# A tail of sixteen chunks: steps of three neighbouring chunks woven between the matmuls of one output tile, and the in-chunk weights by a predicated copy

## The chip, the cores and the metric

The kernel runs on one core of a Trainium2 chip. The metric is the device time of one execution in microseconds (us). TensorE (PE in the profile, PEld its weight loads), VectorE (DVE), ScalarE (ACT), GpSimd (POOL) and the DMA queues issued by SyncE (SP) work in parallel and wait for each other through semaphores.

## The reference, cut to what matters

Two layers of an encoder trunk over 2048 positions of width 1024. Each layer modulates its input, projects it, mixes it in two branches, and ends in `x <- LN(alpha * x + gate * W_out [branch 1 | branch 2])`. The change touches the end of the second layer: its second branch (a bidirectional state-space scan, SSD), its output projection and its last layer norm. What the second branch computes, with the backward direction as the same function on reversed time:

```python
seg = jnp.exp(jnp.where(mask, a_cum[..., :, None] - a_cum[..., None, :], -jnp.inf))
cb = jnp.einsum('bnigs,bnjgs->bgnij', cm, bm)
y = jnp.einsum('bgnij,bgrnij,bnjgrp->bnigrp', cb, seg, x)      # within a chunk
...
y = y + jnp.einsum('bnigs,bgrni,bngrps->bnigrp', cm, jnp.exp(a_cum), s_prev)   # from the carried state
...
x_fw, a_fw = dir_inputs(dt_f, 0)      # xs * dt, dt * -exp(a_log)
x_bw, a_bw = dir_inputs(dt_b, 1)
y = (ssd_chunked(x_fw, a_fw, bm, cm)
     + rev(ssd_chunked(rev(x_bw), rev(a_bw), rev(bm), rev(cm)))
     + d_skip.astype(jnp.float32)[:, None] * xs)
y = rms_norm(y.reshape(bsz, seq, WIDTH_D) * jax.nn.silu(dz.astype(jnp.float32)), ssm_norm_g)
```

Within a chunk of 128 positions both directions are one weight matrix of 128 by 128 for each of 8 heads: `w = E * cb * dt`, with the forward `dt` on one triangle, the backward `dt` on the other, and the sum of both on the diagonal, where `E` is 1.

## The kernel before, in words

The sequence is cut into 16 chunks (`NC`) of 128 positions. When the last input projection is done, these pieces are left, and they are the tail:

- `pass_b` (called through `other`) for two heads of the first branch, segments 1, 2 and 3 of 512 positions each. It ends in a store of the branch's rows of `y`, which the output tiles read back.
- `Ssd.local(c)`, for a chunk: four loads (`tk`, `bc`, `dzl`, `sbl`, lines 1228 to 1235), the product `pcb` (L1238), then for each of two groups of four heads the decay `E = exp(pd)` (POOL and ACT write `rr`, L1246 and L1249; four matmuls `pd`, L1250 and L1251; the exponential, L1253), the `dt` part of the weights (a scaled copy on ACT, L1256, and a `scalar_tensor_tensor` on DVE, L1257, for every head), and two products on DVE (L1259, L1260) that make `w`.
- `Ssd.forward(c)`: the matmuls `py` with `w` (L1273), the skip term (POOL, L1276), two state products `pin` (L1281) each with a DVE product (L1285) and a POOL sum (L1286), the state's update `pu` (L1211, from `xw`, L1203) into `sf` (L1220), the gate (L1292), the norm (L1294 to L1297), four transposes `pt` (L1300) and the result `syo` (L1302).
- `OutProj.steps(c)`, an output tile: 48 matmuls `oo` of 512 columns (L1032), half of them with the first branch's rows (`yr`, read back from memory), half with `syo`; each operand is split in a high part `yH` (L1003) and a low part `yL` (L1004). Then residual, statistics and layer norm (L1039 to L1050) and the store.

The order on each engine is not the written order: the framework plans it when the kernel is built, and of the instructions that are ready it takes the one written earliest. So what is written later fills gaps as far as its inputs and its buffers allow. Many buffers of the tail are single: the two halves of `rr` (tags T0, T1), `E` (cvt), `xw` (v), `syo` (kd), `yL`, and one PSUM bank for `pcb` and `pt` together. The written order before is, in the last loop (L1675 to L1680): `local(c + 1)` whole, at chunks 1, 5 and 9 a `pass_b` whole, `forward(c)` whole, tile c whole.

Of the kernel before, what the change touches and what calls it, by code (L numbers as in the profile page):

```python
# [10 lines left out]
F32 = mybir.dt.float32  # L11
F32R = mybir.dt.float32r
I32 = mybir.dt.int32
AF = mybir.ActivationFunctionType
ALU = mybir.AluOpType
AX = mybir.AxisListType
# [3 lines left out]
P = 128  # L20
# [261 lines left out]
def run(g):  # L282
    for _ in g:
        pass
# [32 lines left out]
def chained(*gs):  # L317
    for g in gs:
        yield from g
# [111 lines left out]
class Rec:  # L431
# [14 lines left out]
    def bank(self, name):  # L446
        return self.ps.tile([P, 512], F32, name=name, tag="rg", bufs=self.e.rg_bufs)
# [613 lines left out]
NC = S // P  # L1061


class Ssd:
# [157 lines left out]
    def local(self, c, pool, bank):  # L1222

        e, nc = self.e, self.e.nc
        cs = slice(c * P, (c + 1) * P)
        k = self.cur[c] = Env()
        kp = self.kp
        k.tk = kp.tile([P, 768], F32, name="tk", tag="tk", bufs=2)
        nc.sync.dma_start(k.tk, self.tok[cs, :])
        k.bc = kp.tile([P, 4, P], F32, name="bc", tag="cvx", bufs=2)  # L1230
        nc.sync.dma_start(k.bc, self.xc[:, :, cs])
        k.dz = kp.tile([P, 512], F32, name="dzl", tag="sb", bufs=2)
        nc.sync.dma_start(k.dz, self.dz[cs, :])
        k.sb = kp.tile([P, 512], F32, name="sbl", tag="cva", bufs=2)
        nc.sync.dma_start(k.sb, self.sbd[c])
        pcb = bank("pcb")
        for g in range(2):
            nc.tensor.matmul(pcb[:, g * P:(g + 1) * P], k.bc[:, g], k.bc[:, 2 + g], start=True, stop=True)  # L1238
        k.w = pool.tile([P, 2, 4, P], F32, name="w", tag="Q", bufs=2)
        for g in range(2):  # L1240
            pd = bank("pd")
            w = k.w[:, g]
            for d, (m1, m2) in enumerate((("gt", "le"), ("lt", "ge"))):
                r = pool.tile([P, 2, 4, P], F32R, name="rr", tag=f"T{d}", bufs=1)
                h0 = d * 8 + g * 4
                nc.gpsimd.tensor_tensor(r[:, 0], e.tri[m2].unsqueeze(1).broadcast_to([P, 4, P]),  # L1246
                                        self.aH[:, c, h0:h0 + 4].unsqueeze(2).broadcast_to([P, 4, P]), ALU.mult)
                for h in range(4):
                    nc.scalar.activation(r[:, 1, h], e.tri[m2], AF.Copy, scale=self.aL[:, c, h0 + h:h0 + h + 1])  # L1249
                nc.tensor.matmul(pd, e.trir[m1], r[:, 0], start=d == 0, stop=False)  # L1250
                nc.tensor.matmul(pd, e.trir[m1], r[:, 1], start=False, stop=d == 1)  # L1251
            E = kp.tile([P, 4, P], F32, name="E", tag="cvt", bufs=1)
            nc.scalar.activation(E, pd.rearrange("p (h i) -> p h i", h=4), AF.Exp)  # L1253
            for h in range(4):
                hh = g * 4 + h
                nc.scalar.activation(w[:, h], e.tri["le"], AF.Copy, scale=self.dt[:, c, hh:hh + 1])  # L1256
                nc.vector.scalar_tensor_tensor(w[:, h], e.tri["ge"], self.dt[:, c, 8 + hh:9 + hh], w[:, h],  # L1257
                                               ALU.mult, ALU.add)
            nc.vector.tensor_tensor(E, E, pcb[:, g * P:(g + 1) * P].unsqueeze(1).broadcast_to([P, 4, P]), ALU.mult)  # L1259
            nc.vector.tensor_tensor(w, w, E, ALU.mult)  # L1260

    def forward(self, c, pool, bank):
        e, nc = self.e, self.e.nc
        cs = slice(c * P, (c + 1) * P)
        h8 = lambda t: t.rearrange("p (h q) -> p h q", h=8)
        k = self.cur.pop(c)
        tk, bc, dz, sb = k.tk, k.bc, k.dz, k.sb
        if c == 0:
            self.sf = pool.tile([P, 512], F32, name="sf", tag="qm0", bufs=1)
            nc.gpsimd.memset(self.sf, 0.0)  # L1270
        py = bank("py")
        for hh in range(8):
            nc.tensor.matmul(py[:, hh * 64:(hh + 1) * 64], k.w[:, hh // 4, hh % 4], tk[:, hh * 64:(hh + 1) * 64],  # L1273
                             start=True, stop=True)
        acc = pool.tile([P, 512], F32, name="yacc", tag=f"{'kq'[c % 2]}m1", bufs=1)
        nc.gpsimd.tensor_tensor(h8(acc), h8(tk[:, :512]), self.dskip.unsqueeze(2).broadcast_to([P, 8, 64]), ALU.mult)  # L1276
        nc.vector.tensor_tensor(acc, py, acc, ALU.add)
        for d, st in ((0, self.sf), (1, sb)):
            po = bank("pin")
            for g in range(2):  # L1280
                nc.tensor.matmul(po[:, g * 256:(g + 1) * 256], bc[:, 2 + g], st[:, g * 256:(g + 1) * 256],  # L1281
                                 start=True, stop=True)
            t = pool.tile([P, 512], F32, name="ti", tag=f"Sf{d}", bufs=1)
            eq = self.ed["qf" if d == 0 else "qb"][:, c, :].unsqueeze(2).broadcast_to([P, 8, 64])
            nc.vector.tensor_tensor(h8(t), h8(po), eq, ALU.mult)  # L1285
            nc.gpsimd.tensor_tensor(acc, acc, t, ALU.add)  # L1286
        if c < NC - 1:
            pu = self.update(self.weighted(c, 0, tk, pool), tk[:, 512:], bank)
            new = pool.tile([P, 512], F32, name="sf", tag=f"{'kq'[c % 2]}m0", bufs=1)
            self.step(new, self.sf, c, 0, pu)  # L1290
            self.sf = new
        nc.vector.tensor_tensor(acc, acc, dz, ALU.mult)  # L1292
        ss = pool.tile([P, 1], F32, name="sss", tag="ss", bufs=4)
        nc.scalar.activation(t, acc, AF.Square, accum_out=ss)  # L1294
        nc.gpsimd.tensor_scalar(ss, ss, 1.0 / 512, 1e-6, ALU.mult, ALU.add)
        nc.gpsimd.tensor_tensor(ss, ss, e.mhalf[:, 0:1], ALU.pow)
        nc.scalar.activation(acc, acc, AF.Copy, scale=ss)  # L1297
        pt = bank("pt")
        for i in range(4):
            nc.tensor.transpose(pt[:, i * P:(i + 1) * P], acc[:, i * P:(i + 1) * P], e.ident)  # L1300
        yo = pool.tile([P, 4, P], F32, name="syo", tag="kd", bufs=1)
        nc.vector.tensor_tensor(yo, pt.rearrange("p (a b) -> p a b", a=4),  # L1302
                                self.gcol.unsqueeze(2).broadcast_to([P, 4, P]), ALU.mult)
        return yo

# [47 lines left out]
def trunk(ctx, tc, i, out):  # L1355
    nc = tc.nc
    e = Env()
# [5 lines left out]
    def const(name, shape, dt=F32):  # L1363
        t = cp.tile(list(shape), dt, name=f"c_{name}")
        nc.sync.dma_start(t, i[name])
        return t
# [63 lines left out]
    mp = opened("gla", "right")  # L1430
# [62 lines left out]
    def others():  # L1493
        for sg in (3, 2, 1, 0):
# [13 lines left out]
    mp = opened("na", "right")  # L1508
# [13 lines left out]
    op = OutProj(e, wp, lambda x, h: wwp.tile([P, ND // 2, D], F32R, name=f"wo{x}{h}"),  # L1522
                 lambda n: wp.tile([P, D], F32, name=n), obank, gated(e, wp, "yr", i["e_w_out"], gate), i["ln_g"][0], i["ln_b"][0], y, i["x"], x1)
# [13 lines left out]
    bank = banks(opened("pt1", "right", space=PSUM), "pt", 4)  # L1537
# [11 lines left out]
    hg = const("hgrn_g", [P, 1])  # L1549
    sg_ = const("ssm_g", [P, 4])  # L1550
    e.tri = {m: const(f"t_{m}", [P, P]) for m in TRI}
    e.trir = {}
    for m in ("gt", "lt"):
        e.trir[m] = cp.tile([P, P], F32R, name=f"r_{m}")
# [24 lines left out]
    kp = opened("conv", "left")  # L1579
    mp = opened("hgrn", "left")  # L1580
# [28 lines left out]
    sd = Ssd(e, sg_, dz, y[512:1024])  # L1609
# [19 lines left out]
    def other(h, sg, tags=None):  # L1629
        return pass_b(e, recs[h:h + 2], sg, mp, bbank, tags or [btags(t, sg % 2) for t in range(2)])  # L1630
# [33 lines left out]
    def sbank(name):  # L1664
# [2 lines left out]

    ftags = [{"qul": ("F", 2), "stwb": ("stw", 1), "sq": ("S320", 1), "og": ("KT", 1)},
             {"qul": ("F", 2), "stwb": ("stwb", 1, wp), "sq": ("S321", 1), "opl": ("uo", 1), "gt": ("q", 1)}]
    sd.local(0, mp, sbank)  # L1670
    sd.local(1, mp, sbank)
    op = OutProj(e, wp, lambda x, h: ip.hp.tile([P, ND // 2, D], F32R, name=f"wo{x}{h}", tag=f"h{'HL'[x]}{h}"),
                 lambda n: mp.tile([P, D], F32, name=n, tag="Kp", bufs=2), obank,
                 wout1, i["ln_g"][1], i["ln_b"][1], y, x1, out)
    for c in range(NC):  # L1675
        if 0 < c < NC - 1:
            sd.local(c + 1, mp, sbank)
        if c % 4 == 1 and c < 12:
            run(other(2, c // 4 + 1, ftags))
        op.tile(c, (4, 8), c == NC - 1, sd.forward(c, mp, sbank))  # L1680
    closed("po1", "pops1", "hp1", "hgrn", "hgrnps", "conv", "wb1", "hgrnc", "ssdc")


def layout(inp):

    f = lambda n: np.ascontiguousarray(inp[n])
    r = {}
# [28 lines left out]
    t, j = a[:, None], a[None, :]  # L1716
    for nm, m in (("gt", t > j), ("lt", t < j), ("le", t <= j), ("ge", t >= j)):
        r["t_" + nm] = m.astype(np.float32)
    lm = np.zeros((P, 5, 32), np.int32)
    i32 = np.arange(32)  # L1720
    for l in range(5):
# [21 lines left out]
```

## Time and profile before

| | us |
|---|---|
| median of 3 runs | 2748.59 (2747.47 to 2750.7) |
| the profiled execution, its own time | 2755.94 |
| its span in the trace | 2754.1 |
| PE busy | 2526.8 (92%) |
| DVE busy | 1493.4 (54%) |
| POOL busy | 1326.1 (48%) |
| ACT busy | 1122.9 (41%) |

Shares are of the whole span. The last matmul of the input projection starts at 2333.37, so the tail is the last 420 us or so. Times in the rows below are us from the span's start unless marked ns; PEclk is the granted TensorE clock as a share of full speed.

### The profile page before, as it was taken

Reading aid. Unit: us, or ns where it says so; the run is one execution under the profiler, and the core shown is the slowest. Engines: PE = TensorE matmul, PEld = TensorE weight load, DVE = VectorE, ACT = ScalarE, POOL = GpSimd, SP = SyncE. Lnnn points to the kernel's source line nnn. Section 1 sums busy time; section 2 is a strip of 40 time slices with the busy share of each in tenths; the row PEclk is TensorE's granted clock in tenths of the full one; section 3 lists DMA queues with packets and bytes.
Section 4 is the critical chain, followed back from the end, with each engine's and each line's share of the span. In section 5 each row is a group of like instructions: output and inputs, shape, how many; then the busy total and the mean of one; then the engine's idle time right before and its main releaser. Section 6 shows DMA issues by size and latency. Waiting matters only on the chain. (4 is left out here: it accounts for less than half of the span.)

```text
span 2754.1 us, 53110 instructions
## 1 busy us (share of the span) xinstructions
PE 2526.8 (92%) x20888; PEld 2125.2 (77%) x20888; DVE 1493.4 (54%) x2493; ACT 1122.9 (41%) x2355; POOL 1326.1 (48%) x1305
## 2 busy tenths in 40 slices
PE   7999999999999799998999999999999888788987
PEld 5877778887778677877788777888877677566776
DVE  6223335124433676765626356432625788687895
ACT  3152323244343644543323444232424453554652
POOL 4252325244442544434535556335534677575874
PEclk9999999999999899999999999999999999798998
DMA  8525434323365878775553335434436567543331
GB/s 275 159 99 169 145 115 132 115 95 106 109 221 181 253 210 234 202 205 167 173 201 126 106 124 177 136 127 131 134 105 207 169 200 235 182 148 112 117 115 62
DMA packets 269800, 432.46 MB, mean 157 GB/s; under 512 B 25936, under 2 KB 143600, under 8 KB 269552
## 3 DMA queue, kind: packets, MB, share of 16 engines
q1 hardware_dynamic: 267248, 420.69, 48.7%
q0 software_dynamic: 2304, 8.39, 0.8%
q8 instruction: 165, 2.70, 0.4%
q14 instruction: 83, 0.68, 0.1%
HBM read 296.60 MB, written 132.38 MB: 156 GB/s over the span
## 5 line engine op out<-in xcount | busy, mean ns | idle before, releaser
L186 POOL TENSOR_TENSOR wl<-wraw,wh 128x1024 fp32r<-128x1024 f32 (+2 forms) x116 | 290.5, 2524 | 293.9 <-ACT wh L185 293.0
L1032 PE MATMUL oo<-wo,yH 128*128 128x512 f32 x1024 | 309.9, 418 | 21.8 <-ACT yH L1003 20.2
L536 POOL TENSOR_TENSOR Kp<-Kp,T 128x256 f32<-128x256 f32 x144 | 125.7, 873 | 275.1 <-ACT F L492 111.7
L1032 PEld LDWEIGHTS oo<-wo,yH 128*128 128x128 f32 x1024 | 199.8, 201 | 65.3 <-ACT yH L1003 23.5
L860 POOL TENSOR_TENSOR nap<-nap,nasm 128x384 f32<-128x384 f32 (+2 forms) x128 | 115.7, 914 | 209.5 <-DVE nasm L859 192.2
L534 DVE TENSOR_TENSOR Kp<-Kp,T 128x256 f32<-128x256 f32 x144 | 103.7, 720 | 146.6 <-PE fine L459 60.2
L185 ACT CAST wh<-wraw 128x1024 fp32r<-128x1024 f32 (+2 forms) x116 | 116.8, 1052 | 154.5 <-PE obqk L205 27.4
L1032 PE MATMUL oo<-wo,yL 128*128 128x512 f32 x512 | 172.4, 405 | 3.0 <-DVE yL L1004 3.0
L532 DVE TENSOR_TENSOR Q<-Q,T 128x512 f32<-128x512 f32 x144 | 146.9, 1020 | 0.0
L885 PE MATMUL nay<-napts,nav 128*128 128x128 f32 (+1 forms) x832 | 121.5, 289 | 20.2 <-ACT napts L872 13.7
L885 PEld LDWEIGHTS nay<-napts,nav 128*128 128x128 f32 (+1 forms) x832 | 114.5, 202 | 31.3 <-ACT napts L872 16.1
L1154 DVE SCALAR_TENSOR_TENSOR cva<-cvx,cw,cva 128x512 f32<-128x512 f32 x96 | 104.2, 1098 | 30.5 <-ACT cva L1152 29.4
L1032 PEld LDWEIGHTS oo<-wo,yL 128*128 128x128 f32 x512 | 97.5, 193 | 23.5 <-DVE yL L1004 4.2
L205 PE MATMUL oqf<-hH,wh 128*128 128x512 f32 x256 | 104.8, 409 | 4.5 <-ACT wh L185 4.5
L205 PE MATMUL ox<-hH,wh 128*128 128x512 f32 x256 | 106.2, 415 | 0.0
L497 DVE COPY_PREDICATED S<-lmask,fine 128x128 f32<-128x128 int32 x160 | 43.7, 297 | 111.3 <-PE fine L459 111.2
L205 PE MATMUL ox<-hH,wl 128*128 128x512 f32 x256 | 102.7, 401 | 0.0
L205 PE MATMUL ox<-hL,wh 128*128 128x512 f32 x256 | 102.5, 400 | 0.0
L205 PE MATMUL oqf<-hL,wh 128*128 128x512 f32 x256 | 102.4, 400 | 0.0
L205 PE MATMUL oqf<-hH,wl 128*128 128x512 f32 x256 | 101.9, 399 | 0.5 <-POOL wl L186 0.5
L858 ACT ACTIVATE nap<-nap,namx 128x384 f32<-128x384 f32 (+2 forms) x128 | 79.2, 619 | 50.6 <-DVE namx L857 50.3
L156 POOL TENSOR_TENSOR hL<-hf,hH 128x512 fp32r<-128x512 f32 x36 | 50.2, 1403 | 96.9 <-ACT hH L155 96.9
(375 smaller groups left out, 7723.8 us busy)
## 6 DMA issues: line engine op xcount, KB each, us to landing
wraw<-in_o_w_dram SPq DMA_DIRECT2D x56, 512.0 KB
wraw<-in_e_w_dram SPq DMA_DIRECT2D x44, 512.0 KB
adw<-in_ada_w_dram SPq DMA_DIRECT2D x32, 512.0 KB
tk<-xtok SPq DMA_DIRECT2D x31, 384.0 KB
nat<-in_na_tab_dram SPq DMA_DIRECT2D x16, 640.0 KB
xt<-in_x_dram SPq DMA_DIRECT2D x16, 512.0 KB
adw<-in_ada_p_dram SPq DMA_DIRECT2D x16, 512.0 KB
naq<-aq SPq DMA_DIRECT2D x64, 128.0 KB
```

The lines of the kernel that those rows point to most:

```text
L156: (nc.vector if d % 2 and not act else nc.gpsimd).tensor_sub(hL[:, d, :], hf, hH[:, d, :].bitcast(F32))
L185: nc.scalar.copy(h[:, sl], raw)
L186: (nc.vector if e.wl_dve else nc.gpsimd).tensor_sub(l[:, sl], raw, h[:, sl].bitcast(F32))
L205: nc.tensor.matmul(oo, a, b, start=d == 0 and m == 0, stop=d == ND - 1 and m == 2)
L532: nc.vector.tensor_tensor(qv, qv, view(tcur, toff + 1, [[nb - 1, 2], [2, n2], [0, s]]), ALU.mult)
L534: nc.vector.tensor_tensor(kv, kv, view(tcur, toff + nb + 1, [[2, n2], [0, s]]), ALU.mult)
L536: nc.gpsimd.tensor_tensor(kv, kv, view(tcur, toff, [[2, n2], [0, s]]), ALU.mult)
L858: nc.scalar.activation(p[:, :nk], p[:, :nk], AF.Exp, bias=mx, scale=-1.0, accum_out=sm)
L860: nc.gpsimd.tensor_tensor(p[:, :nk], p[:, :nk], sm.broadcast_to([P, nk]), ALU.mult)
L885: nc.tensor.matmul(s.yp[:, n, :], b.vs[:kb, n, j, :], s.pts[n][:kb, j, :], start=j == 0, stop=j == nj - 1)
L1032: nc.tensor.matmul(os[n], ops[m][0][:, c, :], ops[m][1][c][:, ns], start=x == 0, stop=x == 23)
L1154: nc.vector.scalar_tensor_tensor(acc, xr[:, k:k + SW], cw[:, i, k:k + 1], acc, ALU.mult, ALU.add)
```

## The change

Four edits, all in the tail:

1. The weights within a chunk. Eight scaled copies (128x128) on ACT and eight `scalar_tensor_tensor` on DVE for a chunk become two copies (128x512) of the backward `dt` on ACT and two `copy_predicated` (128x512) on DVE, which put the forward `dt` where an integer mask `t_lei` is set. The diagonal then has the forward `dt` alone, so the backward `dt` times the diagonal of `pcb` is added to the skip factor: a product with the identity (`own`, DVE, 128x256 out of PSUM), a sum over it (`cd`), and two small products (`k.skip`, 128x8).
2. `local` and `forward` become generators of three steps each; `xw` is made at the end of `local` and not in `forward`.
3. `pass_b` for segments 1 to 3 becomes one generator of 12 steps.
4. The last loop has 17 turns. A turn c writes tile c-1 in its 24 steps of two matmuls, and between them: step 1 of `forward(c)` ahead of the first, step 2 ahead of the third, the three steps of `local(c + 1)` ahead of the 7th, 11th and 15th, one step of `pass_b` ahead of the 13th (turns 1 to 12), and step 3 of `forward(c)` (the transposes) ahead of the 21st.

```diff
@@ -1236,34 +1236,50 @@
         pcb = bank("pcb")
         for g in range(2):
             nc.tensor.matmul(pcb[:, g * P:(g + 1) * P], k.bc[:, g], k.bc[:, 2 + g], start=True, stop=True)
+
+        own = kp.tile([P, 2, P], F32, name="own", tag="cvt", bufs=1)
+        nc.vector.tensor_tensor(own, pcb[:, :2 * P].rearrange("p (g i) -> p g i", g=2),
+                                e.ident.unsqueeze(1).broadcast_to([P, 2, P]), ALU.mult)
+        cd = pool.tile([P, 2], F32, name="cd", tag="cd", bufs=2)
+        nc.vector.tensor_reduce(cd, own, AX.X, ALU.add)
+        k.skip = pool.tile([P, 2, 4], F32, name="skip", tag="skip", bufs=2)
+        nc.vector.tensor_tensor(k.skip, self.dt[:, c, 8:].rearrange("p (g h) -> p g h", g=2),
+                                cd.unsqueeze(2).broadcast_to([P, 2, 4]), ALU.mult)
+        nc.vector.tensor_tensor(k.skip, k.skip, self.dskip.rearrange("p (g h) -> p g h", g=2), ALU.add)
         k.w = pool.tile([P, 2, 4, P], F32, name="w", tag="Q", bufs=2)
         for g in range(2):
-            pd = bank("pd")
             w = k.w[:, g]
-            for d, (m1, m2) in enumerate((("gt", "le"), ("lt", "ge"))):
+            rs = []
+            for d, m2 in enumerate(("le", "ge")):
                 r = pool.tile([P, 2, 4, P], F32R, name="rr", tag=f"T{d}", bufs=1)
                 h0 = d * 8 + g * 4
                 nc.gpsimd.tensor_tensor(r[:, 0], e.tri[m2].unsqueeze(1).broadcast_to([P, 4, P]),
                                         self.aH[:, c, h0:h0 + 4].unsqueeze(2).broadcast_to([P, 4, P]), ALU.mult)
                 for h in range(4):
                     nc.scalar.activation(r[:, 1, h], e.tri[m2], AF.Copy, scale=self.aL[:, c, h0 + h:h0 + h + 1])
-                nc.tensor.matmul(pd, e.trir[m1], r[:, 0], start=d == 0, stop=False)
-                nc.tensor.matmul(pd, e.trir[m1], r[:, 1], start=False, stop=d == 1)
+                rs.append(r)
+            yield
+            pd = bank("pd")
+            for d, m1 in enumerate(("gt", "lt")):
+                nc.tensor.matmul(pd, e.trir[m1], rs[d][:, 0], start=d == 0, stop=False)
+                nc.tensor.matmul(pd, e.trir[m1], rs[d][:, 1], start=False, stop=d == 1)
             E = kp.tile([P, 4, P], F32, name="E", tag="cvt", bufs=1)
             nc.scalar.activation(E, pd.rearrange("p (h i) -> p h i", h=4), AF.Exp)
-            for h in range(4):
-                hh = g * 4 + h
-                nc.scalar.activation(w[:, h], e.tri["le"], AF.Copy, scale=self.dt[:, c, hh:hh + 1])
-                nc.vector.scalar_tensor_tensor(w[:, h], e.tri["ge"], self.dt[:, c, 8 + hh:9 + hh], w[:, h],
-                                               ALU.mult, ALU.add)
+            dts = [self.dt[:, c, d * 8 + g * 4:d * 8 + g * 4 + 4].unsqueeze(2).broadcast_to([P, 4, P]) for d in range(2)]
+            nc.scalar.copy(w, dts[1])
+            nc.vector.copy_predicated(w, e.lei.unsqueeze(1).broadcast_to([P, 4, P]), dts[0])
             nc.vector.tensor_tensor(E, E, pcb[:, g * P:(g + 1) * P].unsqueeze(1).broadcast_to([P, 4, P]), ALU.mult)
             nc.vector.tensor_tensor(w, w, E, ALU.mult)
+        if c < NC - 1:
+            k.xw = self.weighted(c, 0, k.tk, pool)
+        yield
 
     def forward(self, c, pool, bank):
+
         e, nc = self.e, self.e.nc
         cs = slice(c * P, (c + 1) * P)
         h8 = lambda t: t.rearrange("p (h q) -> p h q", h=8)
-        k = self.cur.pop(c)
+        k = self.cur[c]
         tk, bc, dz, sb = k.tk, k.bc, k.dz, k.sb
         if c == 0:
             self.sf = pool.tile([P, 512], F32, name="sf", tag="qm0", bufs=1)
@@ -1273,8 +1289,9 @@
             nc.tensor.matmul(py[:, hh * 64:(hh + 1) * 64], k.w[:, hh // 4, hh % 4], tk[:, hh * 64:(hh + 1) * 64],
                              start=True, stop=True)
         acc = pool.tile([P, 512], F32, name="yacc", tag=f"{'kq'[c % 2]}m1", bufs=1)
-        nc.gpsimd.tensor_tensor(h8(acc), h8(tk[:, :512]), self.dskip.unsqueeze(2).broadcast_to([P, 8, 64]), ALU.mult)
+        nc.gpsimd.tensor_tensor(h8(acc), h8(tk[:, :512]), k.skip.rearrange("p g h -> p (g h)").unsqueeze(2).broadcast_to([P, 8, 64]), ALU.mult)
         nc.vector.tensor_tensor(acc, py, acc, ALU.add)
+        yield
         for d, st in ((0, self.sf), (1, sb)):
             po = bank("pin")
             for g in range(2):
@@ -1285,7 +1302,7 @@
             nc.vector.tensor_tensor(h8(t), h8(po), eq, ALU.mult)
             nc.gpsimd.tensor_tensor(acc, acc, t, ALU.add)
         if c < NC - 1:
-            pu = self.update(self.weighted(c, 0, tk, pool), tk[:, 512:], bank)
+            pu = self.update(k.xw, tk[:, 512:], bank)
             new = pool.tile([P, 512], F32, name="sf", tag=f"{'kq'[c % 2]}m0", bufs=1)
             self.step(new, self.sf, c, 0, pu)
             self.sf = new
@@ -1295,13 +1312,15 @@
         nc.gpsimd.tensor_scalar(ss, ss, 1.0 / 512, 1e-6, ALU.mult, ALU.add)
         nc.gpsimd.tensor_tensor(ss, ss, e.mhalf[:, 0:1], ALU.pow)
         nc.scalar.activation(acc, acc, AF.Copy, scale=ss)
+        yield
         pt = bank("pt")
         for i in range(4):
             nc.tensor.transpose(pt[:, i * P:(i + 1) * P], acc[:, i * P:(i + 1) * P], e.ident)
         yo = pool.tile([P, 4, P], F32, name="syo", tag="kd", bufs=1)
         nc.vector.tensor_tensor(yo, pt.rearrange("p (a b) -> p a b", a=4),
                                 self.gcol.unsqueeze(2).broadcast_to([P, 4, P]), ALU.mult)
-        return yo
+        k.yo = yo
+        yield
 
 
 
@@ -1549,6 +1568,7 @@
     hg = const("hgrn_g", [P, 1])
     sg_ = const("ssm_g", [P, 4])
     e.tri = {m: const(f"t_{m}", [P, P]) for m in TRI}
+    e.lei = const("t_lei", [P, P], I32)
     e.trir = {}
     for m in ("gt", "lt"):
         e.trir[m] = cp.tile([P, P], F32R, name=f"r_{m}")
@@ -1667,17 +1687,23 @@
 
     ftags = [{"qul": ("F", 2), "stwb": ("stw", 1), "sq": ("S320", 1), "og": ("KT", 1)},
              {"qul": ("F", 2), "stwb": ("stwb", 1, wp), "sq": ("S321", 1), "opl": ("uo", 1), "gt": ("q", 1)}]
-    sd.local(0, mp, sbank)
-    sd.local(1, mp, sbank)
+    run(sd.local(0, mp, sbank))
     op = OutProj(e, wp, lambda x, h: ip.hp.tile([P, ND // 2, D], F32R, name=f"wo{x}{h}", tag=f"h{'HL'[x]}{h}"),
                  lambda n: mp.tile([P, D], F32, name=n, tag="Kp", bufs=2), obank,
                  wout1, i["ln_g"][1], i["ln_b"][1], y, x1, out)
-    for c in range(NC):
-        if 0 < c < NC - 1:
-            sd.local(c + 1, mp, sbank)
-        if c % 4 == 1 and c < 12:
-            run(other(2, c // 4 + 1, ftags))
-        op.tile(c, (4, 8), c == NC - 1, sd.forward(c, mp, sbank))
+    second = chained(*(other(2, sg, ftags) for sg in (1, 2, 3)))
+    for c in range(NC + 1):
+        tile_ = op.steps(c - 1, (4, 8), c == NC, sd.cur.pop(c - 1).yo) if c else iter(())
+        fw = sd.forward(c, mp, sbank) if c < NC else iter(())
+        lo = sd.local(c + 1, mp, sbank) if c + 1 < NC else iter(())
+        turns = {0: fw, 2: fw, 6: lo, 10: lo, 14: lo, 20: fw}
+        if 0 < c < 13:
+            turns[12] = second
+        for j in range(24):
+            if j in turns:
+                next(turns[j], None)
+            next(tile_, None)
+        run(tile_)
     closed("po1", "pops1", "hp1", "hgrn", "hgrnps", "conv", "wb1", "hgrnc", "ssdc")
 
 
@@ -1716,6 +1742,7 @@
     t, j = a[:, None], a[None, :]
     for nm, m in (("gt", t > j), ("lt", t < j), ("le", t <= j), ("ge", t >= j)):
         r["t_" + nm] = m.astype(np.float32)
+    r["t_lei"] = (t <= j).astype(np.int32)
     lm = np.zeros((P, 5, 32), np.int32)
     i32 = np.arange(32)
     for l in range(5):
```

## Rows read from the trace of the kernel before

**Rows 1.** Windows of the tail; PE, PEld, DVE, ACT, POOL busy; PEclk, DMA.

```profile
2335.00:2393.00 58.00, 35.44 (x144) 28.65 (x144) 41.07 (x75) 34.73 (x106) 32.82 (x30) 0.70 0.63 221
2393.00:2546.00 153.00, 129.61 (x590) 106.54 (x591) 116.10 (x168) 71.20 (x207) 95.29 (x99) 0.89 0.39 127
2546.00:2711.00 165.00, 150.74 (x731) 124.50 (x729) 143.49 (x205) 92.08 (x260) 116.57 (x116) 0.96 0.35 113
2711.00:2746.00 35.00, 30.48 (x132) 24.07 (x131) 18.76 (x30) 7.91 (x14) 15.36 (x16) 0.90 0.08 30
```

**Rows 2.** Timeline: first output matmul; statistics that end tiles 5 and 13. Start, duration.

```profile
2393.17 1.22 PE L1032 MATMUL oo<-wo,yH 128*128 128x512 f32 x2 [4.22 <-ACT yH L1003]
2546.17 0.69 DVE L1040 BATCH_NORM_STATS2 bst<-r 128x6 f32<-128x512 f32 x1
2711.30 0.68 DVE L1040 BATCH_NORM_STATS2 bst<-r 128x6 f32<-128x512 f32 x1
```

**Rows 3.** Pieces of the chain that ended last: TensorE, and the last residual.

```profile
2529.64 1.27 POOL yacc L1286
...
2612.02 0.84 PE py L1273 x8
2612.85 1.80 PE pin L1281 x8
...
2635.57 0.23 PE pd L1251
...
2636.25 5.49 PE oo L1032 x24
...
2642.14 0.92 PE pu L1211 x4
...
2697.32 0.45 PE pt L1300 x4
...
2745.02 0.70 DVE r L1039
```

**Rows 4.** The same chain, window 2300 to 2755: share by line.

```profile
by line: PE oo L1032 17.0%; DVE w L1257 8.5%; issue 2.5%; PE pin L1281 2.0%; DVE yL L1004 1.3%; DVE r L1048 1.2%; PE py L1273 1.1%; DVE w L1260 1.0%; PE pu L1211 0.9%; DVE yacc L1292 0.9%; ACT rr L1249 0.7%; DVE bst L1040 0.7%; PE pt L1300 
```

**Rows 5.** Groups of instructions by line and shape, window 2393 to 2755.

```profile
L1257 DVE SCALAR_TENSOR_TENSOR w<-c_t_ge,dt,w 128x128 f32<-128x128 f32 x96 | 75.3, 835 | 2.3 <-ACT w L1256 2.3
...
L1256 ACT ACTIVATE w<-c_t_le,dt 128x128 f32<-128x128 f32 x96 | 29.5, 389 | 0.0
...
L1260 DVE TENSOR_TENSOR w<-w,E 128x512 f32<-128x512 f32 x28 | 26.1, 933 | 0.3
...
L1259 DVE TENSOR_TENSOR E<-E,pcb 128x512 f32<-128x512 f32 x28 | 19.0, 677 | 10.4 <-PE pcb L1238 6.5 <-ACT E L1253 3.8
...
L1003 ACT CAST yH<-syo 128x512 fp32r<-128x512 f32 x16 | 9.8, 614 | 24.7 <-DVE syo L1302 24.7
```

**Rows 6.** Lines by source, whole span: duration in ns, least/median/most.

```profile
L1257 DVE SCALAR_TENSOR_TENSOR w<-c_t_ge,dt,w x128: 292/527/1446, 2318.8 to 2687.2; 128x128 f32<-128x128 f32 x128
...
L1260 DVE TENSOR_TENSOR w<-w,E x32: 672/692/1777, 2354.0 to 2713.8; 128x512 f32<-128x512 f32 x32
...
L497 DVE COPY_PREDICATED S<-lmask,fine x160: 274/297/309, 168.1 to 2323.8; 128x128 f32<-128x128 int32 x160
...
L1040 DVE BATCH_NORM_STATS2 bst<-r x32: 678/686/696, 2408.2 to 2745.7; 128x6 f32<-128x512 f32 x32
```

**Rows 7.** Waits, windows from 2380 and 2393; total us, times, longest.

```profile
PE pin L1281 <- DVE sf L1220: 9.8, 4, 3.1
...
POOL rr L1246 <- PE pd L1251: 38.2, 8, 7.3
...
ACT yH L1003 <- DMA yr<-yy: 9.3, 1, 9.3
```

**Rows 8.** Timeline of DVE: a chunk's `forward`, its second and its last DVE step.

```profile
2592.45 0.69 DVE L1277 TENSOR_TENSOR yacc<-py,yacc 128x512 f32<-128x512 f32 x1
...
2611.82 0.69 DVE L1302 TENSOR_TENSOR syo<-pt,c_ssm_g 128x512 f32<-128x512 f32 x1 [1.52 <-PE pt L1300]
```

## The prediction

> **What bounds the kernel now.** The page's shares are of the whole span, so I cut the tail by windows first [rows 1]. The columns to compare are PE busy and the granted clock: their product is about the TensorE work in microseconds at full speed. From the first output matmul at 2393.17 [rows 2] to the last residual at 2745.02 [rows 3] it is 129.61 x 0.89 + 150.74 x 0.96 + 30.48 x 0.90 = 115.4 + 144.7 + 27.4 = 287.5 us in 353 us. So 65.5 us are lost, partly as idle time, partly as work at a lower clock: 37.6 us in the first window (tiles 0 to 5, 6.3 us each), 20.3 in the second (tiles 6 to 13, 2.5 each; their ends lie 165 us apart [rows 2]), 7.6 in the third (tiles 14 and 15).
>
> The work of one steady tile at full speed, from pieces that run back to back [rows 3]: 48 output matmuls 2 x 5.49 = 10.98; eight `pd` 8 x 0.23 = 1.84; sixteen `py` records 2 x 0.84 = 1.68; `pin` 1.80; `pu` 0.92; `pt` 0.45; `pcb`, also four of 128 columns, 0.45. Together 18.1 us. Eight of them are 145 us, which is what the second window shows as work; it took 165.
>
> What fills the rest is DVE: 143.49 of 165 us there, and 116.10 of 153 before [rows 1]. The chain that ended last says the same by line: apart from the output matmuls (17.0%) the largest share is DVE at L1257, 8.5% of the 455 us window, 38.7 us, and all of it after 2529.64, where the chain begins [rows 3, 4]. That line is the eight small `scalar_tensor_tensor` of a chunk. 96 of them kept DVE busy for 75.3 us, 835 ns each with ends that overlap [rows 5], though one can take 292 [rows 6]. The waits of TensorE are spread thin (the longest group, `pin` on the state `sf`, is 9.8 us in four times), and a large wait of POOL, 38.2 us on `pd`, is one for single `rr` buffers [rows 7]. POOL itself is at 71% in the second window, ACT at 56% [rows 1].
>
> **Edit 1, the weights.** Removed for a chunk: 75.3 / 12 = 6.3 us of DVE [rows 5]. Added: two `copy_predicated` of 128x512. The trace has this operation only at 128x128 with data out of PSUM, 0.297 us [rows 6]. Bounds: a column more costs (0.677 - 0.297) / 384, about 1 ns, if L1259 [rows 5] is set against it, so 0.68 us at the least; at the most 1.78, the longest L1260 [rows 6]. I take 0.93, the mean of L1260 [rows 5], which has the same shape and both inputs in SBUF as here. `own` is half an L1259, 0.42; the sum over 256 columns the same by the bn_stats row (0.686 for 512 [rows 6]) less 256 ns, 0.43; the two 128x8 products are smaller than anything here, 0.1 to 0.3 each, taken as 0.2. Added 1.86 + 0.42 + 0.43 + 0.4 = 3.1 us; net 3.2 us of DVE a chunk saved. Ends: 6.3 - 2.6 = 3.7, and 6.3 - 4.8 = 1.5; if the removed ones were as cheap as their least, 2.3 for eight, the edit would cost 0.3 to 2.5. Over the 12 chunks whose weights fall behind 2393 (96 records) 3.2 makes 38 us of DVE. On ACT 8 x 0.389 = 3.1 become two copies at 0.61 [rows 5], 1.9 less; ACT is not the bound, so I cost that at nothing.
>
> The rows show which DVE lines stretch: with both inputs in SBUF (L1257 from 292 to 1446 ns, L1260 from 672 to 1777), while bn_stats, with one, stays within 678 to 696 [rows 6]. The Trainium skill ("SBUF — State Buffer", Who interferes with whom) says that a DVE instruction with two SBUF inputs and a GpSimd instruction that reads SBUF block each other for a whole instruction, and that one with at most one SBUF input, a reduction too, does not; the trace agrees, with the numbers just given. It speaks against part of this edit: the new copy has mask and data in SBUF, so by it the price is nearer 0.93 than 0.68, and the sum 38 us and not 44. No run so far shows the copy in this form.
>
> **Edits 2 to 4, the order.** No matmul, load or store is added or taken away but one load of a 64 KB mask, far ahead of its use; the tail's DMA share is 0.35 to 0.39 once the output weights are in [rows 1], so the loads of `local` and `pass_b`, which move on SP's queue with their steps, cost nothing while it stays so. What moves: `pass_b` came whole at chunks 1, 5 and 9 ahead of `forward`, and now comes in twelve pieces. On TensorE one head of it is twelve records of 128 columns, 3 x 0.45 = 1.35 us by the `pt` row [rows 3], 8.1 us for all six. Before tile 0 nothing of it stands any more. The first output matmul waited for the read-back of the first branch's rows, for which ACT waited 9.3 us [rows 7]; DVE and ACT were 41 and 35 of 58 us busy in that stretch [rows 1]. Between 0 and 9 us are to be had; I take 5, so it starts at 2388. `xw` now stands behind the second group's weights on POOL, and `local(c + 2)` waits for its single buffer, which is free a whole turn earlier; nothing. Behind the transposes of step 3, which wait on ACT, lie the last output matmuls of tile c-1 on TensorE: that is the wait which can come in (below).
>
> At the end the old order left two tiles and most of two `forward` in the last 35 us, 7.6 lost; the new one has tile 15 alone, with `syo` ready.
>
> **The sum.** TensorE work from the first output matmul on: 16 x 10.98 = 175.7; `forward` 1 to 15, 15 x (1.68 + 1.80 + 0.92 + 0.45) = 72.8; `local` 2 to 15, 14 x 2.29 = 32.1; `pass_b` 8.1: 288.7 us. The losses I take at half, between none gone and all gone: six tiles at 3.1, eight at 1.3, 1 for the end: 30 us. The reason for half: in the second window DVE's 17.9 us a tile become 14.7, below TensorE's 18.1, so its cause goes; but POOL's 14.6 [rows 1] remain beside it, and the planned order is not the chip's. Then 2388 + 288.7 + 30 + 9.1 (from the last residual to the end of the span, as now) = 2715.8 against 2754.1: 38 us less. The profiled execution's own time would go from 2755.94 to 2718; the median of the runs lies 7.35 below it, so 2748.59 - 38 = **2710 us**.
>
> **The rivals.**
> - *All of the loss goes* (TensorE bound throughout): 30 us more, 2680. For it: pieces without any gap [rows 3]. Against it: five engines' queues in a fixed order.
> - *Only the lighter DVE counts*, the order brings nothing. L1257 is 38.7 of the chain's last 223 us; 51% (3.2 of 6.3) of that over 360 us is 32 us, and something else takes about half of it: 10 to 25 less, about 2731. For it: the order before already fills gaps from later text.
> - *Nothing moves.* The stalls are of buffers, which the edit does not add: POOL waits 38.2 us for `pd` to free `rr` [rows 7], and these waits set the pace. 2743 to 2754. Against it: POOL has slack there. The Trainium skill ("Perfetto Trace Analysis", Optimization Strategy) says that gaps which repeat can mean too few buffers for the next tile; here the repeated wait is POOL's, and TensorE's are not of one kind.
> - *Slower: `forward` does not fit into a turn.* From its second step to its result it takes 2592.45 to 2611.82, 19.4 us [rows 8]. It now has to run between the first and the 21st of 24 steps of one tile, or the transposes hold TensorE. At 19.4 the turn would be 19.4 x 24 / 20 = 23.3 us. The old time is reached at (2745 - 2388 - 11) / 15 = 23.1 us a turn, 11 being the last tile alone; at 24 it is 14 us slower, 2762. Against it: 3.2 us of the DVE work queued in between goes, and 16.2 x 24 / 20 = 19.4.
>
> **How the numbers follow.** My forecast 0.50 (own range 2694 to 2722), all of the loss 0.08, DVE alone 0.20, nothing 0.09, slower 0.13. A measurement here tells about 0.2% (5.5 us) from no change. Faster: the first three, and a little of the fourth, 0.79; same 0.09; slower 0.12. The range leaves out half of the best case, half of "nothing" and the slower one: 2686 to 2746. The ends of the new copy's price (1.5 to 3.7 us net) move the forecast by about 10 us, half of 1.7 x 12, within it.
>
> **What would show it.** In the profile after: the predicated copy at 0.7 to 1.1 us in 32 records; DVE busy in the tail some 40 us lower; output matmuls in all of the tail with the clock near 1; tile ends about 20 us apart from the first on; the last tile 11 us behind the one before. Wrong if TensorE's waits on `pt` come up in every turn (slower), if the predicated copy takes over 1.5 us, or if tile ends stay 22 us apart with DVE under 75% busy (the order on another engine, POOL first, sets the pace).

## The result, and the profile after

The changed kernel takes 2716.44 us (median of 4 runs, 2711.26 to 2719.07), the kernel before 2749.64 beside it: a ratio of 0.9874, interval 0.9852 to 0.9895, so 33 to 35 us or 1.3% less. The forecast was 2710, the range 2686 to 2746.

The changed kernel from its first output matmul to its last residual, in three windows; columns as in [rows 1]:

```profile
2388.00:2497.00 109.00, 103.40 (x507) 85.79 (x507) 88.12 (x139) 53.29 (x142) 84.66 (x82) 0.97 0.47 149
2497.00:2667.00 170.00, 157.30 (x776) 129.10 (x775) 141.07 (x216) 90.94 (x248) 137.73 (x131) 0.98 0.42 131
2667.00:2709.00 42.00, 39.34 (x189) 31.83 (x187) 25.30 (x43) 13.34 (x27) 23.01 (x23) 1.00 0.14 51
```

PE busy times the clock is 100.3 + 154.2 + 39.3 = 293.8 us of work at full speed in 321 us: 27 us lost, where it was 65.5. The clock, 0.89 to 0.96 before, is 0.97 to 1.00. DVE is at 79% of these 321 us and POOL at 76%; TensorE is busy for 93%. DVE is busy some 24 us less than before (254.5 against 278.4 [rows 1]), but TensorE lost 38 us less: its idle time fell from 42.2 us (353 - 310.8) to 21.0 (321 - 300.0), and what the lower clock cost from 23.3 to 6.2.

The timeline at the first output matmul, and at the statistics that end tiles 0, 5, 12 and 13:

```profile
2387.98 1.20 PE L1032 MATMUL oo<-wo,yH 128*128 128x512 f32 x4 [2.55 <-ACT yH L1003]
...
2407.78 0.68 DVE L1040 BATCH_NORM_STATS2 bst<-r 128x6 f32<-128x512 f32 x1
...
2517.01 0.69 DVE L1040 BATCH_NORM_STATS2 bst<-r 128x6 f32<-128x512 f32 x1
...
2665.35 0.68 DVE L1040 BATCH_NORM_STATS2 bst<-r 128x6 f32<-128x512 f32 x1
...
2682.72 0.69 DVE L1040 BATCH_NORM_STATS2 bst<-r 128x6 f32<-128x512 f32 x1
```

From the end of tile 0 to that of tile 12 it takes 257.6 us, 21.5 a tile, and the ends lie 19.9 to 23.7 us apart, where they lay 13 to 39 apart before. The same span cut as in [rows 1], at the ends of tiles 5 and 13:

```profile
2388.00:2517.00 129.00, 121.25 (x596) 99.79 (x596) 107.08 (x168) 64.73 (x180) 97.94 (x95) 0.97 0.47 149
2517.00:2683.00 166.00, 154.95 (x764) 128.19 (x765) 133.63 (x205) 86.96 (x228) 135.51 (x128) 0.98 0.39 123
2683.00:2709.00 26.00, 23.84 (x109) 18.75 (x108) 13.78 (x24) 5.87 (x10) 11.96 (x12) 1.00 0.11 41
```

Tiles 6 to 13 take 166 us, as before (165). The time is gained in tiles 0 to 5 (129 for 153), in the last two (26 for 35), and at the start, 5 us earlier. The end of the chain that ended last:

```profile
2697.17 11.08 PE oo L1032 x48
...
2708.28 0.70 DVE r L1039
```

The last tile stands alone and without a gap, 11.08 us. The new instructions among the groups by line and shape, from 2388 on:

```profile
L1270 DVE COPY_PREDICATED w<-c_t_lei,dt 128x512 f32<-128x512 int32 x24 | 36.8, 1565 | 0.1
...
L1241 DVE TENSOR_TENSOR own<-pcb,c_ident 128x256 f32<-128x256 f32 x14 | 5.8, 411 | 2.4 <-PE pcb L1238 2.4
L1244 DVE TENSOR_REDUCE cd<-own 128x2 f32<-128x256 f32 x14 | 5.7, 409 | 0.1
...
L1246 DVE TENSOR_TENSOR skip<-dt,cd 128x8 f32<-128x8 f32 x14 | 3.3, 235 | 0.1
...
L1248 DVE TENSOR_TENSOR skip<-skip,dskip 128x8 f32<-128x8 f32 x14 | 2.5, 180 | 0.0
```

Here is a surprise: the predicated copy is not 0.93 us but 1.57. By line its durations (least, median, most) and those of POOL's two sums of `forward`, which had a median of 1312 ns before:

```profile
L1270 DVE COPY_PREDICATED w<-c_t_lei,dt x32: 709/1566/1842, 2319.5 to 2657.2; 128x512 f32<-128x512 int32 x32
```

```profile
L1303 POOL TENSOR_TENSOR yacc<-yacc,ti x32: 1266/1640/1762, 2386.6 to 2692.0; 128x512 f32<-128x512 f32 x32
```

A stretch of the timeline of DVE and POOL shows how both get long:

```profile
2613.71 3.46 POOL L1303 TENSOR_TENSOR yacc<-yacc,ti 128x512 f32<-128x512 f32 x2
2614.24 3.52 DVE L1270 COPY_PREDICATED w<-c_t_lei,dt 128x512 f32<-128x512 int32 x2
2617.66 0.41 DVE L1241 TENSOR_TENSOR own<-pcb,c_ident 128x256 f32<-128x256 f32 x1
```

Two sums and two copies take from 2613.71 to 2617.76, 4.05 us; their least times one after the other are 2 x 1.266 + 2 x 0.709 = 3.95. So the lengths fit sum, copy, sum, copy in turn, the one engine standing with its instruction begun while the other works. Part of the busy time of DVE is here waiting: for the 24 copies of the tail 24 x (1.565 - 0.709), some 20 us of 254.

The largest of TensorE's own waits in the tail, and that for `pt`, from 2388 on (total us, times, longest):

```profile
PE oo L1032 <- ACT yH L1003: 13.4, 12, 2.6
PE py L1289 <- DVE w L1272: 5.5, 6, 1.4
...
PE pt L1318 <- ACT yacc L1314: 0.8, 1, 0.8
```

The wait for the state (9.8 us [rows 7]) is gone. What is left most often, twelve times at about 1.1 us, is the wait for a cast `yH` on ACT. Only four of these casts are of `forward`'s result `syo` (6.0 us). Eight are of the read-back rows `yr` (7.4 us, 2.6 of them ahead of tile 0), and five of the eight stand on ACT right behind the scaling of `forward`'s norm, as here, where that scaling has waited for POOL:

```profile
2470.76 0.72 ACT L1314 ACTIVATE yacc<-yacc,sss 128x512 f32<-128x512 f32 x1 [2.54 <-POOL sss L1313]
2471.39 0.60 ACT L1003 CAST yH<-yr 128x512 fp32r<-128x512 f32 x1
```

### The profile page after: what moved, and what is told of

Same layout as the page of the kernel before. It is cut to its first block, busy times and chain, and to the rows that moved or that the text cites. A ratio compares the mean times of both kernels' runs of the same rounds, so it can differ in the third digit from the quotient of the medians.

```text
span 2717.3 us, 52972 instructions
## 1 busy us (share of the span) xinstructions
PE 2509.4 (92%) x20888; PEld 2113.4 (78%) x20888; DVE 1458.8 (54%) x2461; ACT 1100.4 (40%) x2259; POOL 1341.6 (49%) x1305
## 5 line engine op out<-in xcount | busy, mean ns | idle before, releaser
L1032 PE MATMUL oo<-wo,yH 128*128 128x512 f32 x1024 | 304.0, 410 | 29.1 <-ACT yH L1003 29.1
L1032 PEld LDWEIGHTS oo<-wo,yH 128*128 128x128 f32 x1024 | 193.3, 195 | 70.7 <-ACT yH L1003 34.1
L61 DVE SCALAR_TENSOR_TENSOR acc<-adw,csil,acc 128x1024 f32<-128x1024 f32 x28 | 39.8, 1420 | 107.6 <-DMA adw<-in_ada_w_dram 107.6
```

What stands on the lines that cost most here:

```text
L1032: nc.tensor.matmul(os[n], ops[m][0][:, c, :], ops[m][1][c][:, ns], start=x == 0, stop=x == 23)
```

## The experiments

Ten kernels ran, built from the changed kernel or from the one before by the diffs shown. Medians are of 4 to 6 runs, and the ratio is against the kernel before beside it, whose medians lay from 2749 to 2755; ratios are what to compare across batches.

| | median us | ratio | 95% interval |
|---|---|---|---|
| the change | 2716.4 | 0.9874 | 0.9852 to 0.9895 |
| 1 order only | 2734.9 | 0.9935 | 0.9913 to 0.9957 |
| 2 weights only | 2718.2 | 0.9868 | 0.9852 to 0.9884 |
| 3 weights on ScalarE | 2700.2 | 0.9802 | 0.9779 to 0.9826 |
| 4 copy twice | 2744.1 | 0.9970 | 0.9942 to 0.9998 |
| 5 weights on ScalarE, old order | 2705.7 | 0.9835 | 0.9811 to 0.9859 |
| 6 copies early | 2717.8 | 0.9882 | 0.9845 to 0.9920 |
| 7 pass_b whole | 2714.1 | 0.9866 | 0.9850 to 0.9881 |
| 8 step 3 early | 2717.2 | 0.9878 | 0.9862 to 0.9894 |
| 9 sums on VectorE | 2706.6 | 0.9846 | 0.9816 to 0.9876 |
| 10 ScalarE weights, one sum on VectorE | 2698.4 | 0.9811 | 0.9776 to 0.9847 |

**1. Order only.** My first theory was that the order makes the gain, since the copies had turned out so dear.

```diff
-            nc.scalar.copy(w, dts[1])
-            nc.vector.copy_predicated(w, e.lei..., dts[0])
+            for h in range(4):
+                nc.scalar.activation(w[:, h], e.tri["le"], AF.Copy, scale=self.dt[:, c, hh:hh + 1])
+                nc.vector.scalar_tensor_tensor(w[:, h], e.tri["ge"], self.dt[:, c, 8 + hh:9 + hh], w[:, h], ALU.mult, ALU.add)
```

(and without `own`, `cd` and `k.skip`.)

> The new order with the old weights (eight scaled copies on ScalarE and eight scalar_tensor_tensor on VectorE a chunk, the plain skip factor). Theory O, the order makes the gain: the predicated copies of the changed kernel took 1.57 us each, so the weights edit saves only 6.3 - 3.1 - 1.2 = 2.0 us of VectorE a chunk, some 24 us over twelve chunks, of which less than half is on the path; 2718 to 2728 us. Rival W, the lighter VectorE makes the gain: more than half of the 33 us is lost again, 2733 us or more.

2734.9: only about half of the gain is there, so the theory falls. The tail's window, and the group of the removed line:

```profile
2383.90:2723.00 339.10, 306.76 (x1458) 251.98 (x1456) 292.32 (x410) 169.88 (x480) 232.71 (x232) 0.94 0.38 120
```

```profile
L1261 DVE SCALAR_TENSOR_TENSOR w<-c_t_ge,dt,w 128x128 f32<-128x128 f32 x96 | 86.3, 953 | 0.0
```

The small instructions take 953 ns each where they took 835 [rows 5], and DVE is at 86% of the stretch, where it was at 79%. By this trace the first output matmul is 9.3 us earlier than before, tiles 0 to 5 take 134 us (153 before) and the last two 26 (35), but tiles 6 to 13 take 180 (165).

**2. Weights only.** The other half by itself: the kernel before with edit 1 and nothing else, its loop untouched.

```diff
     for c in range(NC):
         if 0 < c < NC - 1:
             sd.local(c + 1, mp, sbank)      # as before, with copy_predicated and k.skip inside
```

> The old order with the new weights. Theory O: 2740 to 2750 us, the tail's tile ends still uneven. Rival W: below 2733 us. If the two edits need each other, this one is near 2745 and the order alone loses more than half too.

2718.2, as good as the whole change: the rival holds. Its tail's window, and its copies:

```profile
2389.90:2708.20 318.30, 295.77 (x1452) 242.36 (x1452) 247.00 (x384) 157.44 (x417) 242.97 (x234) 0.99 0.39 125
```

```profile
L1266 DVE COPY_PREDICATED w<-c_t_lei,dt x32: 709/733/1840, 2319.6 to 2658.3; 128x512 f32<-128x512 int32 x32
```

In this order half of the copies find the way free (median 733 ns, against 1566). From the first output matmul on, 318 us with 25.5 lost (318.3 - 295.77 x 0.99), against 321 with 27 in the changed kernel. The last two tiles take 26 us here too. With the weights done, the new order brings nothing that can be measured.

**3. Weights on ScalarE.** If queueing on DVE and POOL is the matter, the copy should go altogether. ScalarE can make the `dt` part alone, with the difference of both directions made once ahead:

```diff
-            nc.scalar.copy(w, dts[1])
-            nc.vector.copy_predicated(w, e.lei..., dts[0])
+            for h in range(4):
+                nc.scalar.activation(w[:, h], e.tri["le"], AF.Identity, bias=self.dt[:, c, 8 + hh:9 + hh],
+                                     scale=self.dtd[:, c, hh:hh + 1])
```

> The changed kernel, but the dt part of the weights is made by ScalarE alone: for every head one activation le * (dt_f - dt_b) + dt_b, with the difference made once; no predicated copy. VectorE loses 3.1 us a chunk, ScalarE gains 8 x 0.39 - 2 x 0.65 = 1.8, and GpSimd's sums, 1.59 us each beside the copies, should fall to about 1.3. If the VectorE and GpSimd queues set the pace of the changed kernel: 2698 to 2710 us. If TensorE alone sets it: within 3 us of 2716.

2700.2, 0.7% under the change by the ratios. The tail's window, two of its groups, and the durations of the second:

```profile
2391.40:2691.00 299.60, 289.83 (x1468) 242.63 (x1468) 228.72 (x369) 181.77 (x489) 237.41 (x235) 1.00 0.43 136
```

```profile
L1306 POOL TENSOR_TENSOR yacc<-yacc,ti 128x512 f32<-128x512 f32 x32 | 43.4, 1356 | 5.2 <-DVE yacc L1296 4.3
...
L1272 ACT ACTIVATE w<-c_t_le,dt,dtd 128x128 f32<-128x128 f32 x96 | 38.3, 481 | 0.0
...
L1272 ACT ACTIVATE w<-c_t_le,dt,dtd x128: 477/480/494, 2321.2 to 2641.1; 128x128 f32<-128x128 f32 x128
```

The clock is 1.00, TensorE is busy for 97% of the stretch, POOL's sums are back at 1.36 us, and ScalarE carries 24 us more without harm. So it was not ScalarE's relief that edit 1 paid with. (The activation with two per-partition operands takes 481 ns, the one with one 389; the Trainium skill, "ScalarE: Activation LUTs", What ACT_TABLE_LOAD costs, gives about 93 ns for each such operand, and the trace agrees.)

**4. Copy twice.** How much of a copy reaches the end:

```diff
             nc.vector.copy_predicated(w, e.lei..., dts[0])
+            nc.vector.copy_predicated(w, e.lei..., dts[0])
```

> The changed kernel with each predicated copy issued twice (the same result): two more of them a chunk, 24 to 30 in the tail. If their cost and their hold on the port shared with GpSimd lie on the path, 0.7 to 1.6 us each come back, 2733 to 2755 us; if TensorE covers them, below 2722.

2744.1, three quarters of the gain gone by the ratios. The tail's window:

```profile
2401.60:2747.30 345.70, 309.41 (x1462) 248.00 (x1460) 286.27 (x418) 157.32 (x417) 244.69 (x234) 0.96 0.37 117
```

The time is 27.6 us longer by the medians, 26 by the ratios. The trace is of the longest of six runs, 2758.12, and it starts its output 13.6 us later. In its stretch from the first output matmul to the last residual DVE is busy 32.5 us longer than the 253.8 of the changed kernel, and the stretch is 25.4 us longer (345.7 against 320.3): DVE's queue lies for the most part on the path.

**5. Weights on ScalarE, old order.** Experiment 3's edit in the kernel of experiment 2, so in the loop of the kernel before.

> The old order with the weights made by ScalarE alone (as in the run before that gave 2700 us in the new order). Theory Q: the queues of VectorE and GpSimd, which hold each other up, made the lost time; weights and order each take away part of the same loss. With VectorE freed the order should be worth nothing: 2696 to 2705 us. Rival P: the new order is worth something of its own once VectorE has room: 2710 us or more here.

2705.7, 0.7 us outside of what theory Q said and well short of rival P; its ratio's interval overlaps that of experiment 3. The new order comes out 5.5 us better by the medians and 9 (0.3%) by the ratios, and the intervals leave room for nothing and for twice that; these runs can't tell.

**6. Copies early.** Both copies of a chunk moved into step 1 of `local`.

```diff
         k.w = pool.tile([P, 2, 4, P], F32, name="w", tag="Q", bufs=2)
+        for g in range(2):
+            nc.scalar.copy(k.w[:, g], dts[1])
+            nc.vector.copy_predicated(k.w[:, g], e.lei..., dts[0])
```

> The changed kernel with both scaled copies and both predicated copies of a chunk moved from the second and third step of local into its first. Theory Q: the copies took 1.57 us each because the planned order puts them beside GpSimd's two sums of forward (they took 1.05 in the old order, and 0.71 at the least); moved, they fall to about 1.0 to 1.2 and the sums from 1.58 to about 1.4, 2704 to 2712 us. Rival: the copy is as slow wherever it stands, since GpSimd is busy 77% of the tail; it stays above 1.4 and the time within 4 us of 2716.

2717.8, the tail's copies 1564 ns. These are the rival's figures, but they decide nothing on the copy: the planned order came out the same as the changed kernel's, instruction for instruction on every engine, so the copies stood beside the same sums. What the run gives is a second measurement of the change: 0.9882.

**7. `pass_b` whole** at turns 1, 5 and 9, ahead of the 13th step.

```diff
-        if 0 < c < 13:
-            turns[12] = second
+        if c in (1, 5, 9):
+            turns[12] = chained(other(2, c // 4 + 1, ftags))      # run to its end there
```

> The changed kernel with pass_b whole at turns 1, 5 and 9 and not in twelve pieces. If spreading it is what the new order brings (the old order lost 6.3 us a tile in the stretch that holds it): some 10 to 20 us slower, 2726 to 2736. By theory Q the planner fills gaps with it either way: 2712 to 2721.

2714.1: cutting it in twelve brings nothing.

**8. Step 3 early.**

```diff
-        turns = {0: fw, 2: fw, 6: lo, 10: lo, 14: lo, 20: fw}
+        turns = {0: fw, 2: fw, 6: lo, 10: lo, 14: lo, 17: fw}
```

> The changed kernel with step 3 of forward ahead of the 18th of the 24 steps and not the 21st. TensorE waited 13.4 us in twelve times for the high part made from syo, and only 0.8 us for the transposes' input. If the place of step 3 sets that wait, it goes: 2706 to 2711. If the wait is what the queues of VectorE, GpSimd and ScalarE leave over, it moves to the transposes: 2713 to 2721.

2717.2, and again the planned order came out the same as the changed kernel's, instruction for instruction on every engine. So this says nothing of the place of step 3, but it is a third measurement of the change: 0.9878. The wait of 13.4 us that I had meant to remove is for a cast of `syo` in four of its twelve times only.

**9. Sums on VectorE.** This takes POOL's neighbours away from the copies:

```diff
-            nc.gpsimd.tensor_tensor(acc, acc, t, ALU.add)
+            nc.vector.tensor_tensor(acc, acc, t, ALU.add)
```

> The changed kernel with both sums of forward made by VectorE and not by GpSimd. VectorE gets about 2 x 0.69 us a chunk more (22 us), GpSimd loses 2 x 1.58 (49 us, from 77% busy to about 60%). If the predicated copies took 1.57 us because they and GpSimd's sums hold each other up, they fall to 0.75 to 1.1 us here, and VectorE's busy time hardly grows; time 2708 to 2722. If the copy is that slow in itself, it stays above 1.4 us and the time goes up to 2728 or more.

2706.6, faster than I had said. The copies by line, and the tail's window:

```profile
L1270 DVE COPY_PREDICATED w<-c_t_lei,dt x32: 709/728/1812, 2313.5 to 2643.2; 128x512 f32<-128x512 int32 x32
```

```profile
2383.20:2693.30 310.10, 297.10 (x1468) 245.31 (x1468) 262.65 (x425) 157.32 (x417) 197.07 (x203) 0.98 0.41 132
```

The copy's median goes from 1566 to 728 ns with the copy itself unchanged. In the changed kernel 20 of the tail's 24 copies overlap one of POOL's sums; here 6 of 24 are still over 0.8 us, and each of them overlaps another instruction of POOL. Over the seven traces that have the copy, the 67 copies beside which POOL ran nothing took 709 to 735 ns, and every longer one overlapped an instruction of POOL. DVE takes over both sums of every chunk and is busy only 9 us longer (253.8 before, by the same cut); POOL is busy 48 us less (245.4).

**10. Both remedies.** Experiment 3 with the second of the two sums on VectorE.

> The kernel with the weights made by ScalarE alone, and the second of the two sums of forward on VectorE. There VectorE is busy 229 and GpSimd 237 of 300 us, and TensorE's work at full speed is about 290 of them. If what is left is TensorE's: 2696 to 2704 us, as before. If GpSimd still costs time: 2688 to 2696.

2698.4, the same as experiment 3 within the runs. There TensorE has 289 us of work in 303 (292.28 x 0.99, from 2390.1 to 2693.0), and moving POOL's work brings no more.

## Why the prediction was right, and where it was not

**The time** was right, and so was the place of the loss: 65.5 us lost by TensorE in the tail, of which 27 are left where I had 30. Of the signs that I had named, the clock came to 0.97 to 1.00, and the last tile ends 12.5 us behind the one before (11 said). Tile ends lie 21.5 us apart and not 20, and DVE is busy 24 us less and not 40. The copy at 1.57 us is past the 1.5 that I had called a sign of being wrong; it told of the price of edit 1, below, and not of the time.

**The terms of the sum.** First output matmul at 2388: 2387.98, to the tenth by luck, since the two other traces of the same planned order have 2389.69 and 2393.05. (The reason given, `pass_b` out of the way, is doubtful: weights only, with `pass_b` in the old order, starts at 2389.90.) TensorE's work 288.7: 293.8, though the change adds no matmul; the same product gave 287.5 before, so some of it is the measure's own. Losses 30: 27, but not where I had them: 11, 14 and 2 us in the three windows cut at tiles 5 and 13, for 19, 10 and 1. The stretch from the last residual to the end of the span 9.1: 2717.3 - 2708.28 = 9.0. Together 2715.8 for a span of 2717.3, closer than the terms, since work and losses were off in opposite ways. The forecast of 2710 lies 6 below the median, mostly since I took the profiled execution for 7.35 us over the median, and it was 2.6.

**Edit 1, a term mis-sized.** The copy at 0.93 us, from the L1260 row, is 1.57; `own` and the sum were right (0.41 each for 0.42 and 0.43; 0.42 is not the half of an L1259 row, which is 0.34, but that row less 256 columns at 1 ns), the small ones 0.24 and 0.18 for 0.2. So 6.3 us a chunk became 36.8 / 12 + 0.41 + 0.41 + 0.24 + 0.18 = 4.3 and the saving 2.0, not 3.2, over the tail 24 us of DVE and not 38. The mean stayed under the bound of 1.78, the longest (1.84) did not. The row I took was the mean of an instruction that met POOL only at times; here the plan set 20 of the tail's 24 copies beside a sum of POOL. Experiment 9 shows that it is the neighbour and not the operation. The rule cited in the prediction (the Trainium skill, "SBUF — State Buffer", Who interferes with whom: whole instructions block each other) fits: 4.05 us for two of each, against 3.95 for their least times one after the other. The runs here put the predicated copy with the two-input instructions.

**The step that failed is the share of the order.** I let the lighter DVE and the new order add up, and held "only the lighter DVE counts" for a rival at 2731. It is the case that holds, at a better time: weights alone give 0.9868, the whole change 0.9874, the order alone 0.9935. What I had credited to the order comes with the weights alone: the start is at 2389.90, and the last two tiles take 26 us. The reading that fits the runs, though none isolates it for the order, is that both edits work on the same loss, work queued behind DVE and POOL, which hold each other up. Copying twice lengthens the stretch by 25.4 us for 32.5 us of DVE. That the order brings nothing more beside the weights agrees with the rival's reason: the planner already filled gaps from later text. I rated that reason too low, and took half of DVE's part of the chain to be replaced by something else; it was not. Why the order alone saves 18 us, while its small instructions grow longer, stays open beyond the stretches given with experiment 1; cutting up `pass_b` is not needed once the weights are changed (experiment 7).

**The rivals that fell.** Buffers: POOL's wait for `rr`, 38.2 us [rows 7], is 1.6 us after, in one time, with the same buffers, and 10.8 with the weights alone, in the old order:

```profile
POOL rr L1256 <- PE pd L1265: 1.6, 1, 1.6
```

```profile
POOL rr L1256 <- PE pd L1261: 10.8, 4, 4.1
```

ACT's wait for the same buffers stayed (13.4 us, 12.5 before) while the time fell. So POOL's wait was a result of the pace and not its cause. The slower case: `forward` still takes a whole turn in the chunk shown, from `yacc` at 2586.18 to `syo` at 2607.15:

```profile
2586.18 0.69 DVE L1293 TENSOR_TENSOR yacc<-py,yacc 128x512 f32<-128x512 f32 x1 [0.22 <-PE py L1289]
...
2607.15 0.67 DVE L1320 TENSOR_TENSOR syo<-pt,c_ssm_g 128x512 f32<-128x512 f32 x1
2608.25 0.69 DVE L1293 TENSOR_TENSOR yacc<-py,yacc 128x512 f32<-128x512 f32 x1 [0.42 <-PE py L1289]
```

21 us, and the next chunk's begins 1.1 us later. My 24/20 was wrong, since the transposes need not stand at the written step (experiment 8), and TensorE waited for them only 0.8 us. But the worry was near: of the twelve waits for `yH`, 13.4 us, nine stand behind `forward`'s result or the scaling of its norm. The best case, no loss at all, is nearly reached by experiment 3, with 10 us lost.

## What to carry to other kernels

Where the instructions of two engines lengthen each other, as those of DVE and POOL do here, price an instruction by its neighbours on the other engine: the same copy was 0.73 or 1.57 us. The best single remedy was to give the work to ScalarE, whose instructions kept their length (477 to 494 ns). Two edits that remove the same wait do not add; take each alone before the sum. Where a planner orders the instructions, look at the planned order first, since moving text may change nothing at all, as in experiments 6 and 8.

## What the runs showed that I had not expected

Seen from the end time, a DVE that is busy 79% of a stretch was nearly as good as full: 32.5 us more of it made the stretch 25.4 us longer, and the 25 us that experiment 3 took away gave 16 by the medians, 20 by the ratios. And a predicated copy of 128x512, 709 ns at the least, reaches 1842 with GpSimd at work; GpSimd's sums beside it go from 1312 to 1640 ns in the median.
